# Tile places in SBUF: padded blocks of u, shifted weight halves and reused mask buffers in a hybrid SSD and retention layer

## The chip, the core and the metric

The kernel runs on one core of one Trainium2 chip. The metric is the device time of one execution in microseconds. Before the change, three executions took 860.56, 860.64 and 860.13 us, with a median of 860.56.

## What is computed

One decoder layer on a sequence of 256 tokens with a width of 1024, in fp32. Three blocks follow one another, each behind an RMS norm with a shift and a scale that are computed from a conditioning vector (`ada_w`):

```python
u = modulate(rms_norm(h, norm_ffn1_w), sh1, sc1)
h = h + 0.5 * g1 * swiglu(u, ffn1_w_in, ffn1_w_out)
u = modulate(rms_norm(h, norm_mix_w), sh2, sc2)
h = h + g2 * hybrid_mixer(u, ...)        # SSD branch and retention branch, gated and summed
u = modulate(rms_norm(h, norm_ffn2_w), sh3, sc3)
h = h + 0.5 * g3 * swiglu(u, ffn2_w_in, ffn2_w_out)
out = rms_norm(h, norm_final_w)
```

The projections are matrix products of the 256 tokens with weights of 1024 x 5632 (both FFN inputs), 2816 x 1024 (both FFN outputs), 1024 x 13344 (the mixer's input), 2048 x 1024 twice (the branches) and 1024 x 1024 (the mixer's output).

## The kernel before

**Products.** Activations lie transposed, features on the partitions and the 256 tokens along the free axis. Each fp32 operand is split into a high and a low half of type float32r, and a product is three matmuls on TensorE (`mm3`, lines 134 to 137; `l` is the stationary operand, `r` the moving one):

```python
pe.matmul(o, l[0], r[0], ...)   # L135: high weights, high activations
pe.matmul(o, l[0], r[1], ...)   # L136: high weights, low activations
pe.matmul(o, l[1], r[0], ...)   # L137: low weights, high activations
```

A matmul loads a 128 x 128 stationary tile (a weight load, engine row PEld) and streams the moving operand past it, 256 columns here, 1024 bytes of each partition. While matmul i streams, the weights of matmul i+1 are loaded.

**Weights.** `load` (L113) fetches 1 MB into one of four staging tiles `wst` on SP's queue. `half` (L120 to L128) makes its halves: `act.copy` writes `wh` (L126) and `dve.tensor_tensor` writes `wl` (L127), each 128 x 1024, with four buffers of either (`HALF_BUFS`). All of it comes from the pool `wp`: four `wst`, four `wh`, four `wl`, in this order.

**Activations.** `new_u` (L214) makes `uh` and `ul`, the halves of u, as 8 blocks (one for each 128 features) of T + 2 = 258 columns; a block is 1032 bytes. The two columns more carry the shift, for `early_project` (L257), whose matmuls are 258 columns wide. `pair_project` (L277) is the standard projection of u: 2 tiles of 128 output features x 8 blocks x 3 matmuls. In the first FFN's opening stage (`first_mms`, L415) the loop is turned round: block kt stays for 48 matmuls (16 output tiles x 3), then the next block. In it VectorE also has the dot products of `ada_w` (L179) and the halves of weights and u (L391, L413). The FFN activations are `ah`, `alo`, 22 blocks of 1024 bytes, from a pool `fp` opened once for each FFN; the mixer's tiles of 4 blocks x 1024 bytes are `slot` (name `s`, 17 buffers), from the pool `mx`, at the same base as `fp`. `contract` (L311) multiplies `ah` or a slot with weights, `branch` (L777) a slot. In `v_tile` (L817) and in the second FFN's output (from L974) the roles are turned round: u or `ah` is stationary, `wh` and `wl` move, with 512 or 256 columns.

**Places.** A pool hands out its tiles in the order of their first use, and a later pool begins where the one before ends. In this kernel that gives these starts, in bytes modulo 256:

| tile | before |
|---|---|
| wst, wh, wl (every buffer, and every 128-column slice of them) | 96 |
| uh, block kt | 96 + 8 kt |
| ul, block kt | 160 + 8 kt |
| ah, alo of both FFNs; every block of a slot | 128 |

**Small buffers.** The SSD's tiles `xe`, `st`, `bn` (512 columns) and `ec` (two buffers) serve the steps `states`, `state`, `bc`, `mask_rows` and `back`. The retention's decay masks come in four loads of 128 x 512 into `dm`, which has one buffer (L853 to L855), and `ret_scores` multiplies by them (L862, L863). `dt_tile` has seven small tiles of its own. `wide` is a ring of five buffers of 4 KB. `square_add` (L226) keeps its sum in `ssum`, two buffers.

**Order.** The opening stage is ordered by hand (`manual_schedule`); in the mixer the string `ORDER` gives the order of the steps; inside it each engine's queue, SP's too, is laid out by the tile framework as operands and buffers come free, and then runs in order.

Of the kernel before, what the change touches and what calls it, by code (L numbers as in the profile page):

```python
# [12 lines left out]
F32 = mybir.dt.float32  # L13
F32R = mybir.dt.float32r
# [4 lines left out]
P = 128  # L19
T = 256  # L20
D = 1024
KD = D // P
FFN = 2816
NF = FFN // P
DI = 2048
NH = 32
# [8 lines left out]
V_GB, V_SN, V_RN = 216, 232, 248  # L35
V_DS, V_DTB, V_AL = 264, 280, 312
N_VEC = 344

K_ID, K_TRI, K_M = 0, 128, 256
K_INV, K_SGN = 384, 385  # L40
# [37 lines left out]
def layer(ctx: ExitStack, tc: tile.TileContext, a, out, packing):  # L78
    nc = tc.nc
# [3 lines left out]
    wp = ctx.enter_context(tc.tile_pool(name="wp", bufs=1))  # L83
    sp = ctx.enter_context(tc.tile_pool(name="sp", bufs=1))
    dp = ctx.enter_context(tc.tile_pool(name="dp", bufs=1, space=bass.MemoryType.DRAM))
    pp = ctx.enter_context(tc.tile_pool(name="pp", bufs=4, space=bass.MemoryType.PSUM))
    pm = ctx.enter_context(tc.tile_pool(name="pm", bufs=4, space=bass.MemoryType.PSUM))

    uid = [0]

    def nm(s):
        uid[0] += 1
        return f"{s}_{uid[0]}"
# [51 lines left out]
    al = slice(None)  # L145
# [23 lines left out]
    col = cst.tile([P, N_VEC], F32, name="col")  # L169
# [3 lines left out]
    h = cst.tile([P, KD, T], F32, name="h")  # L173
# [38 lines left out]
        return rs  # L212

    def new_u():  # L214
        full = [sp.tile([P, KD, T + 2], F32R, tag=n, name=nm(n), bufs=1) for n in ("uh", "ul")]
        return tuple(t[:, :, :T] for t in full) + tuple(full)

    def u_tile(u, f, t, jsh):
        sh = modc[:, jsh, f:f + 1]
# [4 lines left out]
    sums = []  # L224

    def square_add(f):  # L226
        if f == 0:
            sums[:] = [sp.tile([P, T], F32, tag="ssum", name=nm("ssum"), bufs=2)]
            act.activation(sums[0], h[:, f, :], AF.Square)
            return  # L230
        sq = sp.tile([P, T], F32, tag="sq", name=nm("sq"), bufs=2)
        act.activation(sq, h[:, f, :], AF.Square)
        if f < KD - 1:
            dve.tensor_tensor(sums[0], sums[0], sq, ALU.add)
        else:
            sums.append(sq)
# [90 lines left out]
    with (tc.tile_pool(name="ep", bufs=1) as ep,  # L327
# [5 lines left out]
        for i in range(2):  # L333
            fetch(h[:, 4 * i:4 * i + 4, :].rearrange("p f t -> p (f t)"), "x",
                  lambda m, i=i: m[:, 512 * i:512 * i + 512].T.reshape(4, P, T).transpose(1, 0, 2))
# [44 lines left out]
        am = sp.tile([P, KD], F32, tag="am", name=nm("am"), bufs=2)  # L380

        def halves(kt):
            his = [wp.tile([P, 1024], F32R, tag="wh", name=nm("wh"), bufs=HALF_BUFS) for _ in range(2)]
            los = [wp.tile([P, 1024], F32R, tag="wl", name=nm("wl"), bufs=HALF_BUFS) for _ in range(2)]
            return his, los

# [82 lines left out]
    with tc.tile_pool(name=nm("fp"), bufs=1, reuse_waits="tile") as fp:  # L469
# [43 lines left out]
        am = scale_col(V_N2, 4)  # L513
# [3 lines left out]
    with tc.tile_pool(name="mx", bufs=1, reuse_waits="tile") as mx:  # L517
# [6 lines left out]
        def small(shape, tag, bufs=1):  # L524
            return mx.tile(shape, F32, tag=tag, name=nm(tag), bufs=bufs)

        def wide(shape, dt=F32):
            return mx.tile(shape, dt, tag="m", name=nm("m"), bufs=WIDE_BUFS)
# [2 lines left out]
        bT, cT = slot([P, 4, T]), slot([P, 4, T])  # L531

        dskip = col[:, V_DS:V_DS + 16]
        dtb, ahead = col[:, V_DTB:V_DTB + NH], small([P, NH], "ahead")
        rows = dp.tile([2, NH, P], F32, name="rows")

        def conv_pair(f0, dst):
# [25 lines left out]
        def dt_tile():  # L563
            need("e")
            st = load(w_in, 0, KD, C_DT, NH)
            wd = wp.tile([P, 1024], F32R, tag="wh", name=nm("wh"), bufs=HALF_BUFS)
            wd = wd[:, :KD * 2 * NH].rearrange("p (k n) -> p k n", k=KD)
            split_into(wd[:, :, :NH], wd[:, :, NH:], st)
            ps = proj_ps()
            for kt in range(KD):  # L570
                uh, ul = at(u, al, kt)
                if kt:
                    pe.matmul(ps[:NH, 0, :], wd[:, kt, :NH], ul, start=False, stop=False)
                pe.matmul(ps[:2 * NH, 0, :], wd[:, kt, :], uh, start=kt == 0, stop=kt == KD - 1)
                if not kt:
                    pe.matmul(ps[:NH, 0, :], wd[:, kt, :NH], ul, start=False, stop=False)
            both = small([2 * NH, NH], "both")
            dve.tensor_tensor(both, ident[:2 * NH, :NH], ident[:2 * NH, NH:2 * NH], ALU.add)
            dtr = wide([2 * NH, T])
            act.copy(dtr, ps[:2 * NH, 0, :])  # L580
            ps = misc_ps()
            for c in range(2):
                pe.matmul(ps[:, c * NH:(c + 1) * NH], dtr[:, c * P:(c + 1) * P], both,
                          start=True, stop=True)
            v, e, s1, s2, pl = (small([P, 2, NH], n) for n in ("dtv", "dte_", "dts", "dts2", "dtp"))
            dve.tensor_tensor(v, ps[:, :64].rearrange("p (c h) -> p c h", c=2),
                              dtb.unsqueeze(1).broadcast_to([P] + x2), ALU.add)
            act.activation(e, v, AF.Abs)
            lookup(ahead, col[:, V_AL:V_AL + NH], AF.Exp)
            lookup(e, e, AF.Exp, scale=-1.0)  # L590
            dve.tensor_scalar(s1, e, 2.0, None, ALU.add)
            dve.reciprocal(s1, s1)
            dve.tensor_tensor(s1, s1, e, ALU.mult)
            dve.tensor_tensor(s2, s1, s1, ALU.mult)
            dve.tensor_scalar(pl, s2, 1.0 / 17, None, ALU.mult)
            for n in (15, 13, 11, 9, 7, 5, 3):
                dve.scalar_tensor_tensor(pl, pl, 1.0 / n, s2, ALU.add, ALU.mult)
            dve.scalar_tensor_tensor(pl, pl, 1.0, s1, ALU.add, ALU.mult)
            dve.tensor_scalar(v, v, 0.0, None, ALU.max)
            dve.scalar_tensor_tensor(dt, pl, 2.0, v, ALU.mult, ALU.add)  # L600
            dve.scalar_tensor_tensor(av, dt, -1.0, ahead.unsqueeze(1).broadcast_to([P] + x2),
                                     ALU.mult, ALU.mult)
# [21 lines left out]
            ps = pair_project(w_in, c0 + p2 * 256, u)  # L624
            lookup(zs[key][:, 2 * p2:2 * p2 + 2, :], ps, AF.Silu)

        bn = small([P, 4, P], "bn")
        cs, dend = small([P, 2, NH], "cs"), small([P, NH], "dend")
        cbs, states, masks = [], {}, {}

# [219 lines left out]

        def ret_scores(hd):
            if hd % 2 == 0:
                dms[hd // 2] = mx.tile([P, 2, T], F32, tag="dm", name=nm("dm"), bufs=1)  # L853
                nc.sync.dma_start(dms[hd // 2].rearrange("p h t -> p (h t)"),
                                  a["dmask"][:, hd * T:(hd + 2) * T])  # L855
            dmask = dms[hd // 2]
            q, kk = qk["q", hd // 4][:, hd % 4, :], qk["k", hd // 4][:, hd % 4, :]
            ps = misc_ps()
            pe.matmul(ps[:, :T], kk[:, :P], q, start=True, stop=True)
            pe.matmul(ps[:, T:T + P], kk[:, P:], q[:, P:], start=True, stop=True)  # L860
            sc = wide([P, T + P])
            dve.tensor_tensor(sc[:, :T], ps[:, :T], dmask[:, hd % 2, :], ALU.mult)  # L862
            dve.tensor_tensor(sc[:, T:], ps[:, T:T + P], dmask[:, hd % 2, :P], ALU.mult)  # L863
            scs[hd] = sc
# [65 lines left out]
        first = modulated(ha, u, 6, "ffn2_w_in", (0, FFN))  # L930
    table("silu_and_others")
    with tc.tile_pool(name=nm("fp"), bufs=1, reuse_waits="tile") as fp:
        ah = fp.tile([P, NF, T], F32R, name=nm("ah"))
        alo = fp.tile([P, NF, T], F32R, name=nm("al"))
        w1 = "ffn2_w_in"
        hN = fp.tile([P, 2, D], F32, name="hN")
        gb = fp.tile([P, D], F32, name="gb")
# [122 lines left out]
```

## Time and profile before

| | |
|---|---|
| median of three executions | 860.56 us |
| profiled execution | 860.98 us |
| its span, first to last instruction | 859.2 us |
| TensorE matmul busy | 846.2 us, 98% |
| VectorE busy | 668.0 us, 78% |
| ScalarE busy | 518.5 us, 60% |
| DMA | 193.14 MB, mean 225 GB/s |

A matmul's duration in the profile overlaps the next one's, so its busy share says little on how fast matmuls follow each other. That pace is read from a stretch: its length divided by the number of matmuls that start in it. A view by windows counts every matmul that is under way in the stretch, and so two more at its start, which began before.

### The profile page before, as it was taken

What the parts mean: (1) busy time and instruction counts of PE and PEld (TensorE: products, weight loads), DVE (VectorE), ACT (ScalarE), POOL (GpSimd) and SP (SyncE); (2) the same over time, 40 slices, a digit from 0 to 9 for tenths busy, and PEclk for the clock granted to TensorE, in tenths of its full rate; (3) what the DMA queues carried; (4) which work ended last, traced back from release to release, by engine and by line L of the source; (5) the groups of instructions that cost most, each with busy time, mean ns of one, the idle gap of its engine ahead of it and who ended that gap; (6) DMA issues with size and microseconds to landing.
All of it is one profiled execution on the core that took longest, in us unless ns stands there. A gap on an engine that the chain in (4) does not pass through costs nothing.

```text
span 859.2 us, 16222 instructions
## 1 busy us (share of the span) xinstructions
PE 846.2 (98%) x6734; PEld 820.4 (95%) x6734; DVE 668.0 (78%) x1002; ACT 518.5 (60%) x743; POOL 10.3 (1%) x21
## 2 busy tenths in 40 slices
PE   7999999999999999999999999999999999999996
PEld 6999999999999989899999999999999999999896
DVE  6989889886989887687897678977979975455463
ACT  6665444465897686766465568765558644545342
POOL 0000000000200010000000000000000000000000
PEclk9999999999999999999999999999999999999999
DMA  9987788984685455435657763654555785454521
GB/s 366 413 325 275 271 296 347 363 319 147 241 313 196 148 209 198 145 135 202 217 176 290 244 219 140 221 194 175 220 194 195 261 305 197 147 192 174 187 87 49
DMA packets 30587, 193.14 MB, mean 225 GB/s; under 512 B 3489, under 2 KB 4129, under 8 KB 10034
## 3 DMA queue, kind: packets, MB, share of 16 engines
q1 hardware_dynamic: 28656, 186.40, 59.6%
q0 software_dynamic: 1568, 5.28, 1.8%
q8 instruction: 52, 0.85, 0.4%
q10 hardware_dynamic: 290, 0.44, 0.1%
q14 instruction: 21, 0.17, 0.1%
HBM read 191.02 MB, written 1.08 MB: 224 GB/s over the span
## 4 chain that ended last, share of the span: by engine, by line
PE 89%; issue 4%; DVE 2%; ACT 2%; DMA 2%; DVEq 0%; ACTq 0%; POOLq 0%
PE proj L137 27%; PE proj L136 27%; PE proj L135 27%; PE misc L135 1%; PE misc L136 1%; PE misc L137 1%; DVE wl L127 1%; DMA k<-in_consts_dram 1%; ACT wh L126 1%; DMA m<-rows 1%; PE misc L727 1%; PE misc L871 1%; PE misc L203 1%; DMA h<-in_x_dram 0%; PE misc L737 0%
## 5 line engine op out<-in xcount | busy, mean ns | idle before, releaser
L126 ACT CAST wh<-wst 128x1024 fp32r<-128x1024 f32 (+1 forms) x263 | 272.9, 1040 | 266.7 <-PE proj L136 178.3
L127 DVE TENSOR_TENSOR wl<-wst,wh 128x1024 fp32r<-128x1024 f32 (+1 forms) x263 | 317.4, 1211 | 133.0 <-ACT wh L126 132.5
L137 PE MATMUL proj<-uh,wl 128*128 128x256 f32 (+1 forms) x1312 | 370.4, 282 | 0.0
L135 PE MATMUL proj<-uh,wh 128*128 128x256 f32 (+1 forms) x1312 | 370.2, 282 | 0.0
L136 PE MATMUL proj<-ul,wh 128*128 128x256 f32 (+1 forms) x1312 | 369.3, 281 | 0.0
L136 PEld LDWEIGHTS proj<-ul,wh 128*128 128x128 f32 x1312 | 248.1, 189 | 0.3 <-issue 0.2
L137 PEld LDWEIGHTS proj<-uh,wl 128*128 128x128 f32 x1312 | 248.2, 189 | 0.2 <-issue 0.2
L135 PEld LDWEIGHTS proj<-uh,wh 128*128 128x128 f32 x1312 | 247.5, 189 | 0.3 <-ACT wh L126 0.2
L135 PE MATMUL proj<-s,wh 128*128 128x256 f32 x320 | 89.9, 282 | 1.0 <-ACT s L793 0.8
L136 PE MATMUL proj<-s,wh 128*128 128x256 f32 x320 | 89.3, 279 | 0.0
L137 PE MATMUL proj<-s,wl 128*128 128x256 f32 x320 | 89.2, 279 | 0.0
L179 DVE SCALAR_TENSOR_TENSOR wst<-wst,cb 128x1024 f32<-128x1024 f32 x56 | 67.0, 1222 | 3.7 <-DMA wst<-in_ada_w_dram 3.6
L135 PEld LDWEIGHTS proj<-s,wh 128*128 128x128 f32 x320 | 60.0, 188 | 2.1 <-ACT s L793 1.6
L136 PEld LDWEIGHTS proj<-s,wh 128*128 128x128 f32 x320 | 60.2, 188 | 0.0
L137 PEld LDWEIGHTS proj<-s,wl 128*128 128x128 f32 x320 | 60.1, 188 | 0.0
L137 PE MATMUL proj<-ah,wl 128*128 128x256 f32 x176 | 49.1, 279 | 0.0
L136 PE MATMUL proj<-al,wh 128*128 128x256 f32 x176 | 49.1, 279 | 0.0
L135 PE MATMUL proj<-ah,wh 128*128 128x256 f32 x176 | 49.1, 279 | 0.0
L136 PE MATMUL proj<-wl,ah 128*128 128x256 f32 (+1 forms) x132 | 42.1, 319 | 0.0
L137 PE MATMUL proj<-wh,al 128*128 128x256 f32 (+1 forms) x132 | 42.1, 319 | 0.0
L135 PE MATMUL proj<-wh,ah 128*128 128x256 f32 (+1 forms) x132 | 42.1, 319 | 0.0
L159 ACT ACT_TABLE_LOAD x30 | 38.5, 1283 | 1.3 <-PEq L1033 0.7
(242 smaller groups left out, 1132.4 us busy)
## 6 DMA issues: line engine op xcount, KB each, us to landing
wst<-in_mix_w_in_dram SPq DMA_DIRECT2D x52, 1024.0 KB, 4.9
wst<-in_ffn_w_in_dram SPq DMA_DIRECT2D x43, 1024.0 KB, 6.5
wst<-in_ada_w_dram SPq DMA_DIRECT2D x28, 1024.0 KB, 6.3
wst<-in_ffn_w_out_dram SPq DMA_DIRECT2D x17, 1024.0 KB, 5.2
ada<-in_ada_w_dram SPq DMA_DIRECT2D x16, 512.0 KB, 12.6
wst<-in_w_br_ssd_dram SPq DMA_DIRECT2D x8, 1024.0 KB, 4.9
wst<-in_w_br_ret_dram SPq DMA_DIRECT2D x8, 1024.0 KB, 5.1
wst<-in_ffn_w_out_dram SPq DMA_DIRECT2D x6, 768.0 KB, 4.5
```

The source lines that it names most:

```text
L126: act.copy(hi, v)
L127: dve.tensor_tensor(lo, v, hi.bitcast(F32), ALU.subtract)
L135: pe.matmul(o, l[0], r[0], start=first, stop=False, skip_group_check=skip)
L136: pe.matmul(o, l[0], r[1], start=False, stop=False, skip_group_check=skip)
L137: pe.matmul(o, l[1], r[0], start=False, stop=last, skip_group_check=skip)
L159: ins = act.preload_act_table_set(name).ins
L179: dve.scalar_tensor_tensor(st[:, i, :], st[:, i, :], 1.0, cb, ALU.mult, ALU.mult, accum_out=raw[:, j, f0 + i:f0 + i + 1])
L203: pe.matmul(ps[:, :T], mean, s, start=i == 0, stop=i == len(parts) - 1)
L727: pe.matmul(py[hh * 64:hh * 64 + 64, f * T + c * P:f * T + (c + 1) * P], xd[:, c, hl * 64:hl * 64 + 64], m[c][:, hl, :], start=True, stop= ...
L871: pe.matmul(py[:, eh, :], v[:, 0, es], sc[:, :T], start=True, stop=False)
```

## The change

The places change, and with them a few tiles. `new_u` makes blocks of 320 columns (1280 bytes) and uses the first 256 or 258. The pool `sp` first hands out its small tiles and a gap of 48 words; `ssum` has one buffer. A gap of 16 words stands between the `wh` and the `wl` tiles. The second FFN's `ah` and `alo` are 24 and 16 words longer, and start behind these. `dt_tile`'s seven small tiles become views of one `wide` tile, and each of the four mask loads has a buffer of its own: `xe`, `st`, `bn` and the second `ec`. Added up, the starts modulo 256 are:

| tile | before | after |
|---|---|---|
| wh | 96 | 96 |
| wl | 96 | 160 |
| uh, block kt | 96 + 8 kt | 0 |
| ul, block kt | 160 + 8 kt | 0 |
| blocks of slots; ah, alo of the first FFN | 128 | 0 |
| ah and alo of the second FFN | 128 and 128 | 96 and 160 |

No matmul and no operation on an engine is added or left out.

```diff
+U_ROW = 320
...
+    for tag, n, bufs in (("am", KD, 2), ("g", KD, 2), ("eb", 4, 1), ("gap", 48, 1)):
+        sp.tile([P, n], F32, tag=tag, name=tag, bufs=bufs)
...
     def new_u():
-        full = [sp.tile([P, KD, T + 2], F32R, tag=n, name=nm(n), bufs=1) for n in ("uh", "ul")]
-        return tuple(t[:, :, :T] for t in full) + tuple(full)
+        full = [sp.tile([P, KD, U_ROW], F32R, tag=n, name=nm(n), bufs=1) for n in ("uh", "ul")]
+        return tuple(t[:, :, :T] for t in full) + tuple(t[:, :, :T + 2] for t in full)
...
-            sums[:] = [sp.tile([P, T], F32, tag="ssum", name=nm("ssum"), bufs=2)]
+            sums[:] = [sp.tile([P, T], F32, tag="ssum", name=nm("ssum"), bufs=1)]
...
             his = [wp.tile([P, 1024], F32R, tag="wh", name=nm("wh"), bufs=HALF_BUFS) for _ in range(2)]
+            if kt == 0:
+                wp.tile([P, 16], F32, tag="gap", name="wgap")
             los = [wp.tile([P, 1024], F32R, tag="wl", name=nm("wl"), bufs=HALF_BUFS) for _ in range(2)]
...
-        dtb, ahead = col[:, V_DTB:V_DTB + NH], small([P, NH], "ahead")
+        dtb = col[:, V_DTB:V_DTB + NH]
...
-            both = small([2 * NH, NH], "both")
+            work = wide([P, 12, NH])
+            both, ahead = work[:2 * NH, 10], work[:, 11]
...
-            v, e, s1, s2, pl = (small([P, 2, NH], n) for n in ("dtv", "dte_", "dts", "dts2", "dtp"))
+            v, e, s1, s2, pl = (work[:, 2 * i:2 * i + 2] for i in range(5))
...
-        bn = small([P, 4, P], "bn")
+        bn = small([P, 512], "bn").rearrange("p (g n) -> p g n", g=4)
...
             if hd % 2 == 0:
-                dms[hd // 2] = mx.tile([P, 2, T], F32, tag="dm", name=nm("dm"), bufs=1)
-                nc.sync.dma_start(dms[hd // 2].rearrange("p h t -> p (h t)"),
-                                  a["dmask"][:, hd * T:(hd + 2) * T])
+                dm = small([P, 512], ("xe", "st", "bn", "ec")[hd // 2], 2 if hd == 6 else 1)
+                nc.sync.dma_start(dm, a["dmask"][:, hd * T:(hd + 2) * T])
+                dms[hd // 2] = dm.rearrange("p (h t) -> p h t", h=2)
...
-        ah = fp.tile([P, NF, T], F32R, name=nm("ah"))
-        alo = fp.tile([P, NF, T], F32R, name=nm("al"))
+        ah, alo = (fp.tile([P, NF * T + n], F32R, name=nm(name))[:, n:]
+                   .rearrange("p (f t) -> p f t", f=NF) for name, n in (("ah", 24), ("al", 16)))
```

## Rows read from the trace of the kernel before

**Rows 1.** The page's part 1: busy us (share of the span), instructions

```profile
PE 846.2 (98%) x6734; PEld 820.4 (95%) x6734; DVE 668.0 (78%) x1002; ACT 518.5 (60%) x743; POOL 10.3 (1%) x21
```

**Rows 2.** Waits of PE, all: line, releaser, us in total, times, longest us

```profile
PE misc L365 <- DMA crow<-in_c_dram: 2.3, 1, 2.3
PE misc L373 <- DVE bn L376: 1.2, 1, 1.2
PE misc L435 <- DVE dg L432: 0.9, 1, 0.9
PE proj L135 <- ACT s L793: 0.8, 1, 0.8
PE misc L203 <- ACT sq L232: 0.3, 1, 0.3
PE proj L135 <- ACT s L131: 0.2, 1, 0.2
```

**Rows 3.** Groups by line and form on PE: out<-moving,stationary, count | busy us, mean ns

```profile
L137 PE MATMUL proj<-uh,wl 128*128 128x256 f32 x1280 | 361.4, 282 | 0.0
L137 PE MATMUL proj<-s,wl 128*128 128x256 f32 x320 | 89.2, 279 | 0.0
L137 PE MATMUL proj<-ah,wl 128*128 128x256 f32 x176 | 49.1, 279 | 0.0
...
L137 PE MATMUL misc<-uh,wl 128*128 128x256 f32 x64 | 18.0, 281 | 0.0
...
L137 PE MATMUL misc<-uh,wl 128*128 128x258 f32 x32 | 9.1, 284 | 0.0
```

**Rows 4.** Windows: stretch, length, busy of PE, PEld, DVE, ACT, POOL; clock, DMA

```profile
672.21:729.25 57.04, 57.04 (x482) 57.04 (x481) 42.44 (x58) 27.93 (x34) 0.00 (x0) 1.00 0.73 261
452.69:504.03 51.34, 51.34 (x434) 51.34 (x433) 38.51 (x47) 26.99 (x34) 0.00 (x0) 1.00 0.69 248
142.16:203.75 61.59, 61.59 (x530) 61.59 (x529) 49.79 (x76) 31.59 (x47) 0.00 (x0) 1.00 0.81 296
418.64:429.84 11.20, 11.20 (x98) 11.20 (x97) 9.04 (x11) 6.31 (x8) 0.00 (x0) 1.00 0.67 238
...
789.80:820.58 30.78, 30.78 (x134) 24.79 (x133) 15.06 (x14) 12.09 (x12) 0.00 (x0) 1.00 0.52 178
```

**Rows 5.** Windows of the opening stage: blocks 1, 2, 4, 5, 6 of u

```profile
22.17:27.92 5.75, 5.75 (x50) 5.75 (x49) 5.46 (x10) 3.46 (x7) 0.00 (x0) 1.00 1.03 415
27.93:33.63 5.70, 5.70 (x50) 5.70 (x49) 5.40 (x9) 4.25 (x7) 0.00 (x0) 1.00 1.03 419
...
39.40:45.05 5.65, 5.65 (x50) 5.65 (x49) 5.35 (x9) 3.70 (x6) 0.00 (x0) 1.00 1.01 409
45.06:50.84 5.78, 5.78 (x50) 5.78 (x49) 5.48 (x10) 3.69 (x6) 0.00 (x0) 1.00 1.02 418
50.85:56.51 5.66, 5.66 (x50) 5.66 (x49) 5.36 (x9) 3.70 (x6) 0.00 (x0) 1.00 0.70 252
```

**Rows 6.** Timeline of PE: first and last of dt_tile's 16 matmuls

```profile
216.22 0.28 PE L574 MATMUL proj<-uh,wh 128*64 128x256 f32 x1
...
217.97 0.28 PE L574 MATMUL proj<-uh,wh 128*64 128x256 f32 x1
```

**Rows 7.** The chain in order of time: transposes, 128 columns each

```profile
742.56 1.75 PE misc L970 x16
```

**Rows 8.** Timeline of DVE: low half of blocks 1 and 7 of u

```profile
20.74 0.43 DVE L413 TENSOR_TENSOR ul<-uf,uh 128x256 fp32r<-128x256 f32 x1 [0.30 <-ACT uh L409]
...
54.63 0.43 DVE L413 TENSOR_TENSOR ul<-uf,uh 128x256 fp32r<-128x256 f32 x1 [0.30 <-ACT uh L409]
```

**Rows 9.** Waits of SP's queue: the mask loads

```profile
SPq L854 <- DVE m L863: 15.8, 3, 5.8
```

**Rows 10.** The tile ec: its last reader, first and last start

```profile
L740 DVE TENSOR_TENSOR s<-s,ec x4: 682/688/691, 309.0 to 415.5; 128x512 f32<-128x512 f32 x4
```

**Rows 11.** The tile dm: the products with the masks, first and last start

```profile
L862 DVE TENSOR_TENSOR m<-misc,dm x8: 413/420/426, 504.9 to 582.6; 128x256 f32<-128x256 f32 x8
```

## The prediction

> **What bounds the kernel now.** I read the page's busy shares first: TensorE's matmuls fill 98% of the span, the weight loads 95%, VectorE 78%, ScalarE 60% [rows 1]. Then PE's waits: six of them, 5.7 us in all, 4.4 us of it in the first three, before the products begin [rows 2]. So the time is the number of matmuls times the pace at which they follow each other, and the change adds and removes none. The one question is whether places change the pace.
>
> The pace comes from the windows, length over matmuls started (the count less the two that were under way). The projections of u run at 57.04 us / 480 = 118.8 ns and 51.34 / 432 = 118.8 ns; the first FFN's contraction, with `ah` moving, at 61.59 / 528 = 116.65 ns; a branch, with slots moving, at 11.20 / 96 = 116.7 ns [rows 4]. [...] What differs is the place: `ah` and slots start at 128 modulo 256, every block, against weights at 96, while each block of u stands 8 bytes further than the one before.
>
> The opening stage separates place from the rest, because one block of u stays for 48 matmuls. Its windows take 5.75, 5.70, 5.65, 5.78 and 5.66 us for blocks 1, 2, 4, 5 and 6, so 119.8, 118.8, 117.7, 120.4 and 117.9 ns [rows 5]. Same code, same engines beside it, another address: up to 2.7 ns. The odd blocks, at 8 modulo 16, are the slow ones.
>
> The second part of the cause is the weight load. `dt_tile` multiplies the very same unaligned blocks of u with stationary tiles of 64 and 32 columns instead of 128; its 16 matmuls take 217.97 - 216.22 = 1.75 us for 15 steps, 116.7 ns [rows 6]. With a short weight load beside it, u has no penalty. So I read the extra 2.2 ns as the stream of u and the weight load meeting in SBUF, and 116.65 ns as the pace of 256 moving columns left alone. The second FFN's output agrees: with 512 columns for one weight load it takes 30.78 us / 132 = 233.2 ns, twice 116.6 [rows 4].
>
> [...]
>
> **The change part by part.** *u at 0 modulo 256, weights at 96 and 160.* 256-column matmuls with u moving: 1280 and 64 for each of three lines, so 4032; 258-column ones: 32 to `misc`, as many to `proj`, on three lines, so 192 [rows 3]. No row shows u at 0 against 96 or 160. Bounds for the new pace: from above the worst block, 120.4 ns [rows 5]; from below the weight load alone, which in the transposes of 128 columns paces 1.75 us / 16 = 109.4 ns [rows 7]. I take 116.65, because the two arrangements that stay the same over many matmuls (slots, `ah`) and the one with hardly a weight load all lie there. That gives (4032 + 192) x (118.8 - 116.65 = 2.15 ns) = 9.1 us less.
>
> *Slots and the first `ah`, `alo` from 128 to 0.* 320 x 3 + 176 x 3 = 1488 matmuls [rows 3], already at 116.65. I take 0. The bounds are those of u: 1488 x 3.75 = 5.6 us more, or, a third of the way down to 109.4, at 114.2 ns, 1488 x 2.45 = 3.6 us less.
>
> *Second FFN's output and `v_tile`.* Here weights move, at 96 and 160, and the stationary tiles go to 96/160 and 0. By the code these are 132 of 512 columns and 264 of 256, and 192 of 512 columns, 106 us at the paces above. Nothing tells a sign; I take 0. The bounds are 114.2 and 120.4 ns per 256 columns, so 2.2 us less to 3.4 us more.
>
> *VectorE as the cover.* In the opening stage the low half of block 1 ends at 20.74 + 0.43 = 21.17 us, 1.0 us before its first matmul, and these halves come every (54.63 - 20.74) / 6 = 5.65 us [rows 8]. At 116.65 ns a block takes 5.60 us, so the lead shrinks by 0.3 us and holds: no cost. Below 114.2 ns (5.48 us, six blocks times 0.17 us) it is used up and VectorE sets this stage.
>
> *Mask loads.* Four loads as before. Three of them now wait in SP's queue for VectorE's reads of the single `dm`, 15.8 us in all, with weight loads behind them [rows 9], yet PE waits for none of it [rows 2]; with four buffers that wait goes, and is worth 0. The new buffers' readers must be done first; `ec`, the last, is read until 415.5 + 0.7 us [rows 10], and the first product with a mask starts at 504.9 us [rows 11]. *`dt_tile` in the ring, one `ssum`, the gaps.* No instruction more; one buffer of the ring is taken earlier. At worst a wait like PE's longest in the mixer, 0.8 us [rows 2]; I take 0.
>
> **Sum.** The profiled execution took 860.98 us; less 9.1 gives 851.9. The median of the runs is 0.4 us below the profiled one, so 851.5 us.
>
> **The rivals.** *Slower: the new distance is a bad one.* Everything that moves from 0 (4224 of u, 1488 of slots and `ah`) falls into step with the weight load as the odd blocks do. At 119.8 ns, block 1's pace, u loses 4224 x 1.0 = 4.2 us and the rest 1488 x 3.15 = 4.7 us: 869.5 us. It decides from a common pace of 118.2 ns upwards, the mean over both kinds today ((4224 x 118.8 + 1488 x 116.65) / 5712). For it: the even blocks scatter too (118.8, 117.7, 117.9), so alignment is not all. Against it: the slowest rows, blocks 1 and 5, start at 8 modulo 16, and the new place never does.
>
> [...]
>
> *Faster than forecast.* 116.65 ns is itself a meeting of the two streams, in all of today's arrangements, and the new distances avoid more of it. At 114.2 ns the gain is another 5712 x 2.45 = 14.0 us: 837.5 us, where VectorE begins to bind in the opening stage. For it: the weight load alone paces 109.4 ns [rows 7]. Against it: 512 columns per load run no better than 256.
>
> **How the numbers follow.** Forecast 0.50 (about 847 to 856 us, with the bounds of the places that I set to 0), faster than that 0.22, no change 0.13, slower 0.15. So faster by over 0.2% (1.7 us, about what a measurement of this kernel can tell from no change) 0.72, same 0.13, slower 0.15. The range runs from 838, the rival's 114.2 ns, to 861, which takes in no change; it leaves out the slower case and some 0.05 below.
>
> **What would show it.** Right: windows over projections of u and over slots have one pace, near 116.7 ns; the opening stage's blocks are all alike, about 5.60 us; PE's waits stay near 6 us; the mask loads wait for nothing. Wrong: the blocks are alike but at 118 ns or more (the distance is what counts, not the alignment); u's pace unchanged with its scatter (the cause was never the place); slots below 116 ns (the third rival); or PE waits for VectorE's halves in the opening stage, the new bound.

## The result and the profile after

The changed kernel took 856.23 us, the median of six executions (854.66 to 856.98), against 860.6 us for six of the kernel before (860.1 to 861.15): a ratio of 0.9949, 95% interval 0.9939 to 0.996. It is 4.4 us faster. The forecast was 851.5 us, 9.1 us faster, so the direction was right and a good half of the gain is missing. The profiled execution took 856.98 us, the slowest of the six, and 4.0 us less than the profiled one of before.

The page's part 1 after the change; the instructions are as many as in [rows 1]:

```profile
PE 842.5 (99%) x6734; PEld 816.4 (95%) x6734; DVE 667.5 (78%) x1002; ACT 519.2 (61%) x743; POOL 10.3 (1%) x21
```

The waits of PE, the four longest of six (line, releaser, us in total, times, longest; the change moves line numbers, so `mm3` is now L139 to L141):

```profile
PE misc L369 <- DMA crow<-in_c_dram: 2.3, 1, 2.3
PE misc L377 <- DVE bn L380: 1.2, 1, 1.2
PE proj L139 <- ACT s L800: 0.8, 1, 0.8
PE misc L441 <- DVE dg L438: 0.5, 1, 0.5
...
```

With two more of 0.2 us that is 5.2 us against 5.7 [rows 2]: the kernel is bound as it was, by the pace of its matmuls. Windows of the changed kernel (columns as in [rows 4]): u in the first FFN, `ah`, u in the mixer's first part, a branch with slots, u behind it, u in the second FFN, the second FFN's first output with 512 columns:

```profile
17.89:141.54 123.65, 123.65 (x1047) 123.65 (x1046) 111.47 (x163) 70.11 (x96) 0.00 (x0) 1.00 0.85 325
141.54:204.02 62.48, 62.48 (x530) 62.48 (x529) 50.03 (x76) 31.93 (x47) 0.00 (x0) 1.00 0.78 292
228.76:287.35 58.59, 58.59 (x508) 58.59 (x508) 52.74 (x84) 49.27 (x94) 5.97 (x10) 1.00 0.69 240
439.41:450.50 11.09, 11.09 (x98) 11.09 (x97) 11.09 (x15) 5.37 (x6) 0.00 (x0) 1.00 0.68 230
450.50:500.42 49.92, 49.92 (x434) 49.92 (x433) 38.68 (x49) 26.99 (x34) 0.00 (x0) 1.00 0.71 257
668.93:725.74 56.81, 56.81 (x482) 56.81 (x481) 42.41 (x58) 27.96 (x34) 0.00 (x0) 1.00 0.73 262
786.01:816.53 30.52, 30.52 (x134) 24.81 (x133) 15.03 (x14) 12.09 (x12) 0.00 (x0) 1.00 0.53 177
```

The expected single pace near 116.7 ns is not there; there are two. In the first FFN u runs at 123.65 / 1045 = 118.3 ns and `ah` at 62.48 / 528 = 118.3 ns (before: 116.65 [rows 4]); in the second FFN u is at 56.81 / 480 = 118.4. The branch takes 11.09 / 96 = 115.5 ns and u behind it 49.92 / 432 = 115.6 (before: 116.7 and 118.8). The granted clock was 1.00 in all seven windows, as in those of [rows 4]. The opening stage's blocks are now alike, which they were not in [rows 5]:

```profile
22.26:27.94 5.68, 5.68 (x50) 5.68 (x49) 5.38 (x10) 3.14 (x7) 0.00 (x0) 1.00 1.02 422
...
39.30:44.98 5.68, 5.68 (x50) 5.68 (x49) 5.38 (x10) 3.70 (x6) 0.00 (x0) 1.00 1.00 411
...
50.66:56.34 5.68, 5.68 (x50) 5.68 (x49) 5.38 (x8) 3.70 (x6) 0.00 (x0) 1.00 0.60 212
```

5.68 / 48 = 118.3 ns, every block behind the first. And the pace changes at a seam. The timeline of PE around 500.4 us, where two score matmuls of the retention stand between two projections (start, us, engine, line, operation):

```profile
500.08 0.28 PE L139 MATMUL proj<-uh,wh 128*128 128x256 f32 x1
500.19 0.28 PE L140 MATMUL proj<-ul,wh 128*128 128x256 f32 x1
500.31 0.28 PE L141 MATMUL proj<-uh,wl 128*128 128x256 f32 x1
500.42 0.59 PE L866 MATMUL misc<-s,s 128*128 128x256 f32 x2
...
501.43 0.28 PE L139 MATMUL proj<-uh,wh 128*128 128x256 f32 x1
501.55 0.29 PE L140 MATMUL proj<-ul,wh 128*128 128x256 f32 x1
501.68 0.28 PE L141 MATMUL proj<-uh,wl 128*128 128x256 f32 x1
501.80 0.28 PE L139 MATMUL proj<-uh,wh 128*128 128x256 f32 x1
```

Three matmuls take 0.34 to 0.35 us ahead of them and 0.37 us just behind; the 18 after those, to 503.93 us, take 2.13 us, 118.3 ns each: same operand places, another pace.

**Where the 4.0 us come from.** Start to next start, added up by kind over each profiled execution, before against after: 256-column matmuls over u 481.9 to 476.6 us, the 258-column ones 24.0 to 23.8, so 5.5 us less on u; slots 113.66 to 114.46 and `ah` 61.60 to 62.48, so 1.7 us more; `v_tile` and the second FFN's output together 0.2 us less. Of the gain on u 4.4 us lie in the mixer between 204 and 500.7 us, where the pace is near 115.6 ns. The opening stage's 384 matmuls gain nothing: they take 46.6 us in both executions. Its blocks 1 to 7 gain 0.3 us, and the first one loses 0.4, where nine matmuls instead of five follow each other at 0.21 us; those behind them follow at 0.12.

### The profile page after: what moved, and what is told of

Read it like the earlier page. It is cut to its first block, busy times and chain, and to the rows that moved or that the text cites. A ratio compares the mean times of both kernels' runs of the same rounds, so it can differ in the third digit from the quotient of the medians.

```text
span 854.9 us, 16219 instructions
## 1 busy us (share of the span) xinstructions
PE 842.5 (99%) x6734; PEld 816.4 (95%) x6734; DVE 667.5 (78%) x1002; ACT 519.2 (61%) x743; POOL 10.3 (1%) x21
## 4 chain that ended last, share of the span: by engine, by line
PE 91%; issue 4%; DMA 2%; ACT 2%; DVE 1%; DVEq 0%; ACTq 0%; POOLq 0%
PE proj L139 28%; PE proj L141 27%; PE proj L140 27%; PE misc L139 1%; PE misc L141 1%; PE misc L140 1%; DMA k<-in_consts_dram 1%; DMA m<-rows 1%; PE misc L734 1%; PE misc L207 1%; PE misc L878 1%; ACT wh L130 0%; DMA h<-in_x_dram 0%; PE misc L744 0%; ACT s L171 0%
## 5 line engine op out<-in xcount | busy, mean ns | idle before, releaser
L139 PE MATMUL proj<-uh,wh 128*128 128x256 f32 (+1 forms) x1312 | 369.3, 281 | 0.0
L141 PE MATMUL proj<-uh,wl 128*128 128x256 f32 (+1 forms) x1312 | 368.0, 280 | 0.0
L141 PEld LDWEIGHTS proj<-uh,wl 128*128 128x128 f32 x1312 | 248.2, 189 | 0.2 <-issue 0.2
L139 PEld LDWEIGHTS proj<-uh,wh 128*128 128x128 f32 x1312 | 247.1, 188 | 0.3 <-ACT wh L130 0.2
L139 PE MATMUL proj<-s,wh 128*128 128x256 f32 x320 | 90.2, 283 | 1.0 <-ACT s L800 0.8
L141 PE MATMUL proj<-s,wl 128*128 128x256 f32 x320 | 89.6, 280 | 0.0
L139 PEld LDWEIGHTS proj<-s,wh 128*128 128x128 f32 x320 | 60.0, 188 | 2.1 <-ACT s L800 1.7
L141 PEld LDWEIGHTS proj<-s,wl 128*128 128x128 f32 x320 | 60.5, 189 | 0.0
L139 PE MATMUL proj<-ah,wh 128*128 128x256 f32 x176 | 49.5, 281 | 0.0
L141 PE MATMUL proj<-ah,wl 128*128 128x256 f32 x176 | 49.4, 281 | 0.0
L139 PE MATMUL proj<-wh,ah 128*128 128x256 f32 (+1 forms) x132 | 42.1, 319 | 0.0
L141 PE MATMUL proj<-wh,al 128*128 128x256 f32 (+1 forms) x132 | 41.8, 317 | 0.0
```

What stands on the lines that cost most here:

```text
L139: pe.matmul(o, l[0], r[0], start=first, stop=False, skip_group_check=skip)
L141: pe.matmul(o, l[1], r[0], start=False, stop=last, skip_group_check=skip)
```

## The experiments

All edits below are against the changed kernel. First came the question which part of the change acts, and whether alignment or distance does. "Distance" is the start of the moving operand less the start of `wh`, modulo 256; the second number of a pair is the start of `wl` less that of `wh`. So slots and `ah` before were at 32/0, and everything that moves is now at 160/64.

**The small buffers alone.** All large places as before:

```diff
-U_ROW = 320
+U_ROW = 258
...
-    for tag, n, bufs in (("am", KD, 2), ("g", KD, 2), ("eb", 4, 1), ("gap", 48, 1)):
-        sp.tile([P, n], F32, tag=tag, name=tag, bufs=bufs)
...
-            if kt == 0:
-                wp.tile([P, 16], F32, tag="gap", name="wgap")
...
-                   .rearrange("p (f t) -> p f t", f=NF) for name, n in (("ah", 24), ("al", 16)))
+                   .rearrange("p (f t) -> p f t", f=NF) for name, n in (("ah", 0), ("al", 0)))
```

> The small buffers alone (four mask buffers, dt_tile's tiles in the ring, one ssum), all large places as before: wh, wl at 96, blocks of u at 96 and 160 plus 8 kt, slots and ah at 128. If the places carry the whole change: 860.6 us within 0.8, u at 118.8 ns, slots and ah at 116.7 ns. If the small buffers carry part of the 4.4 us (three waits of SP's queue fewer): 856 to 859 us at the same paces.

Measured: 860.2 us, ratio 0.9997 (0.9988 to 1.0007). u again takes 57.23 / 481 = 119.0 ns and `ah` 61.59 / 528 = 116.65. Mask loads, `dt_tile`'s ring tile and `ssum` are worth nothing that this run can tell from zero; the places carry the change.

**Everything that moves at 128, `wl` back at 96**, so u, slots and `ah` all at the 32/0 that slots and `ah` had before:

```diff
-    for tag, n, bufs in (("am", KD, 2), ("g", KD, 2), ("eb", 4, 1), ("gap", 48, 1)):
+    for tag, n, bufs in (("am", KD, 2), ("g", KD, 2), ("eb", 4, 1), ("gap", 32, 1)):
...
-            if kt == 0:
-                wp.tile([P, 16], F32, tag="gap", name="wgap")
...
-                   .rearrange("p (f t) -> p f t", f=NF) for name, n in (("ah", 24), ("al", 16)))
+                   .rearrange("p (f t) -> p f t", f=NF) for name, n in (("ah", 0), ("al", 0)))
```

> Blocks of u (1280 bytes apart), slots and every ah at 128, wh and wl both at 96. Theory distance (what counts is how far the moving operand stands from the next weights; 128 to 96 is a good distance, 0 to 96 and 160 a middling one): u, slots and ah all at 116.7 ns or a little below, so 4224 x 2.15 = 9.1 us under before, 851.5 us. Theory alignment (any constant place gives u about 117.3 ns, and slots lost by something else in the change): u stays at 117.3 ns, slots and ah go back to 116.7 ns, 854.5 us.

Measured: 854.15 us, ratio 0.9922 (0.9908 to 0.9937), better than the change itself. Its windows: u in the first FFN, `ah`, u in the mixer:

```profile
56.09:140.30 84.21, 84.21 (x717) 84.21 (x716) 75.19 (x111) 44.31 (x54) 0.00 (x0) 1.00 0.82 299
140.30:202.49 62.19, 62.19 (x530) 62.19 (x529) 49.90 (x76) 31.66 (x47) 0.00 (x0) 1.00 0.80 294
449.78:500.18 50.40, 50.40 (x434) 50.40 (x433) 38.58 (x47) 26.98 (x34) 0.00 (x0) 1.00 0.69 254
```

117.8, 117.8 and 116.7 ns. `ah` stands modulo 256 just where it stood before, against the same weights, and takes 62.19 us instead of 61.59 [rows 4]. So a place does not have one pace: what I had taken from slots and `ah` as the pace of a place was one of its paces. Neither expectation held: the time is near that of the alignment theory, 854.5 us, but the paces are those of neither.

**`wl` back at 96 alone**, u, slots and `ah` at 0 (160/0):

```diff
-    for tag, n, bufs in (("am", KD, 2), ("g", KD, 2), ("eb", 4, 1), ("gap", 48, 1)):
+    for tag, n, bufs in (("am", KD, 2), ("g", KD, 2), ("eb", 4, 1), ("gap", 64, 1)):
...
-            if kt == 0:
-                wp.tile([P, 16], F32, tag="gap", name="wgap")
```

> The changed kernel with wl back at 96, so that wh and wl both stand at 96 and u, slots and ah at 0. If the shift of wl to 160 is what cost slots and ah 1.0 and 1.7 ns: they are back at 116.7 ns, and the time is 853.8 to 854.5 us. If it is the distance from 0 to 96: they stay near 118 ns, and the time is 856.2 us or, where 160 was chosen well, above it, up to 860 us.

Measured: 859.71 us, ratio 0.9989 (0.9975 to 1.0003). Its ten executions lie between 856.44 and 862.43 us; nineteen of the kernel before, on the same chip, between 859.79 and 861.26. The profiled one is the 856.44 of them, with stretches at two paces (u in the first FFN, and in the second):

```profile
56.15:139.57 83.42, 83.42 (x712) 83.42 (x712) 74.75 (x110) 43.59 (x54) 0.00 (x0) 1.00 0.82 301
740.30:785.75 45.45, 45.45 (x385) 45.45 (x384) 23.39 (x23) 22.33 (x27) 0.00 (x0) 1.00 0.50 178
```

711 and 383 matmuls start in them behind the first: 117.3 and 118.7 ns. Slots and `ah` did not go back to 116.7 ns (`ah` runs at 117.3), so the shift of `wl` is not all that cost them their pace. By the medians that shift was worth 3.5 us of the change's 4.4, but the fastest execution at 160/0 lies among those of the change.

**Everything at 96** (0/0):

```diff
-    for tag, n, bufs in (("am", KD, 2), ("g", KD, 2), ("eb", 4, 1), ("gap", 48, 1)):
+    for tag, n, bufs in (("am", KD, 2), ("g", KD, 2), ("eb", 4, 1), ("gap", 24, 1)):
...
-            if kt == 0:
-                wp.tile([P, 16], F32, tag="gap", name="wgap")
...
-                   .rearrange("p (f t) -> p f t", f=NF) for name, n in (("ah", 24), ("al", 16)))
+                   .rearrange("p (f t) -> p f t", f=NF) for name, n in (("ah", 0), ("al", 0)))
```

> Everything at 96: blocks of u, slots, every ah, wh and wl, so that the distance is 0. Theory distance: as block 0 of u did in the opening stage of the kernel before (uh at 96 beside weights at 96, 119.2 ns and, once periodic, 120.0), all of u, slots and ah at 119 to 120 ns, so 5700 x 1.5 to 2 over the mean of 118.2: 865 to 871 us. Theory alignment: u 117.3, slots and ah 116.7 to 118 ns, 854 to 857 us.

Measured: 867.66 us, ratio 1.0084 (1.0067 to 1.0101), slower than before. Its windows: `ah`, u in the mixer, 512 columns in the second FFN:

```profile
142.68:206.04 63.36, 63.36 (x530) 63.36 (x529) 50.07 (x76) 31.90 (x47) 0.00 (x0) 1.00 0.77 288
456.53:508.37 51.84, 51.84 (x434) 51.84 (x433) 38.11 (x47) 26.90 (x34) 0.00 (x0) 1.00 0.66 242
796.95:826.90 29.95, 29.95 (x134) 24.78 (x133) 14.98 (x14) 12.11 (x12) 0.00 (x0) 1.00 0.54 178
```

63.36 / 528 and 51.84 / 432 are both 120.0 ns, as the theory of distance expected, and so is every other long stretch of 256 columns. Each block is aligned here as in the change, so alignment is not what pays: with it the blocks become alike, at whatever pace the distance gives (118.3 ns in the change, 120.0 here). The 512-column matmuls gain at the same time (226.9 ns, before 233.2 [rows 4]): a place that was bad for 256 columns was good for 512. The weights move in these, but the role is not what decides: the 256-column matmuls of the same output, weights moving too, stay at 120.0 ns here.

**A row of matmuls alone.** A kernel that computes nothing of the layer: three matmuls as in `mm3`, twelve times over, for each distance of the moving operand (0 to 240 in steps of 16) and of `wl` (0 to 224 in steps of 32), and each pair three times: right behind the last, behind one 512-column matmul, behind a 128-column matmul of fp32, a form that the trace shows as two (`ones` by `ones` in the kernel before, L352: eleven in the code, 22 in the trace). No other engine has work then. Further rows of the same kernel move all operands together, and exchange the roles at 512 columns.

```diff
...
+        for lo in range(0, 64, 8):
+            for d in range(0, 64, 4):
+                for n in range(3):
+                    kick(n)
+                    triples(12, d, 0, (0, lo))
...
```

> None of the layer is computed here: the kernel is a row of matmuls alone, groups of 36 (12 of the three-matmul products, 256 columns), with no other engine at work. The distance from wh to the moving operand goes through 0 to 240 bytes in steps of 16, that from wh to wl through 0 to 224 in steps of 32, and each pair runs three times: straight on, behind a 512-column matmul, and behind two 128-column fp32 ones. At the end some pairs repeat with both weights moved by 32, 64 and 96 bytes. Theory rhythm (the two streams lock into one of a few periodic patterns, which the distances allow and the interruption before the group picks): the pairs of the kernels run so far show their paces here too: 120.0 ns at 0/0; 116.7 and 117.8 at 32/0; 117.3 and 118.7 at 160/0; 115.6 and 118.3 at 160/64; and some pairs give different paces behind different interruptions. Theory other engines (the scatter within one kernel comes from what ScalarE, VectorE and DMA do beside): one pace for each pair, the same behind all three. Shifting everything together changes nothing if distances alone count.

Measured at 256 columns over the last 23 steps of each row of 36, in ns (distance/`wl`, the three repetitions):

| pair | where | ns |
|---|---|---|
| 0/0 | all at 96 | 120.0, 120.0, 120.0 |
| 32/0 | slots, `ah` before | 116.7, 116.8, 116.8 |
| 160/0 | `wl` back at 96 | 118.8, 118.7, 118.9 |
| 160/64 | the change | 118.5, 118.3, 118.3 |
| 192/0 | | 113.3, 117.8, 113.3 |
| 64/128 | | 113.3, 118.9, 113.3 |
| 192/128 | | 113.3, 113.3, 113.3 |
| 96/224 | the worst | 124.7, 124.7, 117.7 |

Windows of that kernel, from the 13th matmul of a row to its last start: 0/0 once, 64/0 twice (behind nothing, and behind the 512-column matmul), 160/64 once, 192/128 once:

```profile
42.15:44.91 2.76, 2.76 (x25) 2.76 (x24) 0.00 (x0) 0.00 (x0) 0.00 (x0) 1.00 0.00 0
...
90.49:93.09 2.61, 2.61 (x25) 2.61 (x24) 0.00 (x0) 0.00 (x0) 0.00 (x0) 1.00 0.00 0
94.85:97.56 2.71, 2.71 (x25) 2.71 (x24) 0.00 (x0) 0.00 (x0) 0.00 (x0) 1.00 0.00 0
...
597.14:599.86 2.72, 2.72 (x25) 2.72 (x24) 0.00 (x0) 0.00 (x0) 0.00 (x0) 1.00 0.00 0
...
1046.48:1049.09 2.61, 2.61 (x25) 2.61 (x24) 0.00 (x0) 0.00 (x0) 0.00 (x0) 1.00 0.00 0
```

Length over 23 gives 120.0, 113.5, 117.8, 118.3 and 113.5 ns. VectorE, ScalarE and GpSimd stand at 0.00 and DMA at 0, and most paces of the layer are there all the same, 113.3, 116.7, 117.8, 118.3, 118.9 and 120.0 ns: no other engine is needed for them. The rhythm theory of the expectation held in part. At 64/0 the same matmuls at the same places run at two paces, and the difference is what ran just before; 36 of the 128 pairs differ by more than 0.5 ns between their repetitions. But 160/0 does not show the layer's 117.3 ns, nor 160/64 its 115.6. Moving all operands by 32, 64 or 96 bytes together left 120.0 at 0/0 (and 120.0 to 120.2 at 96/0), and 116.5 to 117.8 at 32/0, the two paces that the layer has there: it is the distance that counts. With the roles exchanged 512 columns take 226.6 to 235.7 ns by place, 227.4 at 0/0. Nor do busy engines change the 120.0 ns at 0/0: it is the same here, with none of them at work, and in the layer, beside 50.07 us of VectorE and 31.90 of ScalarE in 63.36 us, and DMA at 288 GB/s.

**Theory from here on: a rhythm.** This is my reading of the paces above; no view shows where the two streams meet. At a given distance the moving stream and the weight loads fall into one of a few repeating patterns; an interruption (a stall, another kind of matmul, the border of a stage) picks which, and it holds until the next. Then 192/128, one of three pairs with the low pace in all three repetitions (112/0 and 16/128 are the others), should do best in the layer, and pairs with two paces should show both.

**192/128 in the layer**: u, slots and `ah` at 32, `wl` at 224:

```diff
-    for tag, n, bufs in (("am", KD, 2), ("g", KD, 2), ("eb", 4, 1), ("gap", 48, 1)):
+    for tag, n, bufs in (("am", KD, 2), ("g", KD, 2), ("eb", 4, 1), ("gap", 40, 1)):
...
-                wp.tile([P, 16], F32, tag="gap", name="wgap")
+                wp.tile([P, 32], F32, tag="gap", name="wgap")
...
-                   .rearrange("p (f t) -> p f t", f=NF) for name, n in (("ah", 24), ("al", 16)))
+                   .rearrange("p (f t) -> p f t", f=NF) for name, n in (("ah", 16), ("al", 0)))
```

> The changed kernel with other places: u, slots and the first ah at 32, wh at 96, wl at 224, the second FFN's ah and alo at 96; so u stands 192 behind wh and wl 128 behind wh, a pair that ran at 113.3 ns in the row of matmuls after all three interruptions. Theory rhythm: u, slots and ah at 113.3 to 113.6 ns over whole stretches; from before, 4224 x 5.4 + 1488 x 3.3 = 28 us less, 832.5 us, and up to 5 us of that given back where VectorE's halves become the bound (opening stage): 832 to 838 us. If the row of matmuls does not stand for the kernel (the other engines disturb, and each interruption throws it into 117.7 ns): 850 to 855 us.

Measured: 840.09 us (838.53 to 840.79), ratio 0.9763 (0.9749 to 0.9778): faster than both kernels, though 2.1 us above the 838 expected at most. Its windows (u in the first FFN, in the mixer, in the second FFN, and 512 columns):

```profile
56.40:136.99 80.58, 80.58 (x712) 80.58 (x712) 72.46 (x109) 43.56 (x54) 0.00 (x0) 1.00 0.83 300
...
443.46:492.42 48.96, 48.96 (x434) 48.96 (x433) 38.99 (x49) 26.98 (x34) 0.00 (x0) 1.00 0.72 264
657.42:711.84 54.42, 54.42 (x482) 54.42 (x481) 42.34 (x58) 27.97 (x34) 0.00 (x0) 1.00 0.75 272
769.78:800.57 30.79, 30.79 (x134) 24.79 (x133) 15.07 (x14) 12.05 (x12) 0.00 (x0) 1.00 0.52 181
```

48.96 / 432 = 113.3 ns, and 113.3 to 113.4 in the others: in every long stretch of 256 columns with u, slots or `ah` moving the pace that the row alone has. The opening stage hardly gains by it. Its blocks 1 to 3:

```profile
21.37:26.81 5.44, 5.44 (x50) 5.44 (x49) 5.14 (x9) 3.67 (x6) 0.00 (x0) 1.00 1.02 413
26.81:32.25 5.44, 5.44 (x50) 5.44 (x49) 5.14 (x8) 3.59 (x6) 0.00 (x0) 1.00 1.02 414
32.25:37.87 5.62, 5.62 (x50) 5.56 (x49) 5.32 (x9) 3.69 (x6) 0.00 (x0) 1.00 1.03 419
```

Two blocks go through at 5.44 us (113.3 ns); the third begins with a gap of 0.14 us, and blocks 3 to 6 take 5.62, 5.63, 5.77 and 5.60 us, 5.66 on average. That is the rate of VectorE's low halves of u, and in each of these blocks the second matmul, the first that reads `ul`, starts 0.05 us after VectorE has ended that block's half (32.39 and 32.34 us in block 3). The tile `ul` in the same run, first and last start:

```profile
L419 DVE TENSOR_TENSOR ul<-uf,uh x8: 424/426/427, 15.0 to 54.6; 128x256 fp32r<-128x256 f32 x8
```

39.6 / 7 = 5.66 us, as in [rows 8]. Blocks 1 to 7 together take 39.45 us, after the change 7 x 5.68 = 39.76; at 113.3 ns throughout they would take 38.1. New among PE's waits is also one for `wl`, in the first FFN's contraction:

```profile
PE proj L141 <- DVE wl L131: 1.3, 3, 0.8
```

So part of the gain becomes waits for VectorE. These three did not change the pace: `ah` is at 113.3 ns ahead of the first (137.1 to 154.8 us) and behind the last (178.1 to 197.9).

**192/0 in the layer**: u, slots and `ah` at 32, `wl` at 96:

```diff
-    for tag, n, bufs in (("am", KD, 2), ("g", KD, 2), ("eb", 4, 1), ("gap", 48, 1)):
+    for tag, n, bufs in (("am", KD, 2), ("g", KD, 2), ("eb", 4, 1), ("gap", 8, 1)):
...
-            if kt == 0:
-                wp.tile([P, 16], F32, tag="gap", name="wgap")
...
-                   .rearrange("p (f t) -> p f t", f=NF) for name, n in (("ah", 24), ("al", 16)))
+                   .rearrange("p (f t) -> p f t", f=NF) for name, n in (("ah", 16), ("al", 0)))
```

> As d32wl224 with wl at 96: distance 192, wl 0 behind wh, a pair that ran at 113.3, 117.8 and 113.3 ns after the three interruptions. Theory rhythm: within one execution some stretches at 113.3 and others at 117.8 ns, the change falling on an interruption, so anything from 834 to 856 us, and executions that differ by several us, as those with u at 0 and wl at 96 did. Theory of one pace for each place: all stretches of u alike, executions within 1 us.

Measured: 846.38 us, ratio 0.9835 (0.9821 to 0.985). The two paces of the row alone, 113.3 and 117.8, stand side by side. Windows of the same contraction of `ah`, first and second part, and the timeline of PE between them:

```profile
137.04:167.00 29.96, 29.96 (x267) 29.96 (x266) 25.89 (x41) 13.27 (x19) 0.00 (x0) 1.00 0.94 342
173.34:198.43 25.09, 25.09 (x214) 25.09 (x214) 18.43 (x27) 14.12 (x22) 0.00 (x0) 1.00 0.67 251
```

```profile
172.40 0.28 PE L139 MATMUL proj<-ah,wh 128*128 128x256 f32 x1
172.52 0.28 PE L140 MATMUL proj<-al,wh 128*128 128x256 f32 x1
173.12 0.38 PE L141 MATMUL proj<-ah,wl 128*128 128x256 f32 x1 [0.32 <-DVE wl L131]
173.34 0.28 PE L139 MATMUL proj<-ah,wh 128*128 128x256 f32 x1
173.46 0.28 PE L140 MATMUL proj<-al,wh 128*128 128x256 f32 x1
173.57 0.28 PE L141 MATMUL proj<-ah,wl 128*128 128x256 f32 x1
```

113 ns up to 172.5 us (29.96 us for 264 or 265 matmuls); then one wait of 0.32 us for VectorE; then 25.09 / 213 = 117.8 ns to the end of the stage, from the first matmuls on. Operands and places are those from before the wait. VectorE and DMA are less busy behind it (18.43 of 25.09 us and 251 GB/s, against 25.89 of 29.96 and 342), but the row alone had both paces at 192/0 with either idle. The stall itself costs 173.34 - 172.52 less two steps, 0.6 us; the pace that it leaves behind 213 x 4.45 ns = 0.9 us.

**64/128 in the layer**: u, slots and `ah` at 160, `wl` at 224:

```diff
-    for tag, n, bufs in (("am", KD, 2), ("g", KD, 2), ("eb", 4, 1), ("gap", 48, 1)):
+    for tag, n, bufs in (("am", KD, 2), ("g", KD, 2), ("eb", 4, 1), ("gap", 8, 1)):
...
-                wp.tile([P, 16], F32, tag="gap", name="wgap")
+                wp.tile([P, 32], F32, tag="gap", name="wgap")
...
-                   .rearrange("p (f t) -> p f t", f=NF) for name, n in (("ah", 24), ("al", 16)))
+                   .rearrange("p (f t) -> p f t", f=NF) for name, n in (("ah", 48), ("al", 0)))
```

> u, slots and the first ah at 160, wh at 96, wl at 224: distance 64, wl 128 behind, a pair that ran at 113.3, 118.9 and 113.3 ns. Theory rhythm: stretches at 113.3 and at 118.9 ns side by side, 834 to 862 us, executions apart by several us. Theory of one pace for each place: as for the run before.

Measured: 854.26 us, ratio 0.9929 (0.9912 to 0.9946): 118.89 ns in the first FFN and most of the mixer, 113.34 in the second FFN. Windows in the two FFNs:

```profile
56.09:144.90 88.81, 88.81 (x749) 88.81 (x749) 79.22 (x116) 46.53 (x57) 0.00 (x0) 1.00 0.81 296
...
741.58:779.65 38.07, 38.07 (x338) 38.07 (x337) 21.03 (x20) 19.27 (x22) 0.00 (x0) 1.00 0.53 189
```

88.81 / 747 and 38.07 / 336: again the two paces that the row alone showed for this pair, 118.9 and 113.3. The rhythm theory's other sign, executions several us apart, did not come: the four lie within 1.4 us here, and within 2.8 at 192/0.

**Narrow stationary tiles, alone.** This tests the sentence of the prediction that a short weight load leaves the moving columns alone. The row of matmuls again, none of the layer, with stationary tiles of 32, 64 and 128 columns:

```diff
...
+        for c in (32, 64, 128):
+            for d in (0, 8, 16, 28, 40, 48):
...
+                    narrow(16, d, c)
...
```

> A row of matmuls alone again, none of the layer. First part: wh and wl at one place, the stationary tile 32, 64 or 128 columns wide, the moving operand 0, 32, 64, 112, 160 or 192 bytes behind, 48 matmuls after each of the three interruptions. If 116.7 ns is what 256 moving columns take alone, as the prediction had it: 32 and 64 columns run at 116.7 ns at every distance, and only 128 columns differ by distance (120.0 at 0, 113.3 or 117.8 at 64 and 192). If the pace is made by the meeting with the weight load and nothing else: the narrower the tile, the lower the pace, towards 109 ns at 32 columns, and no distance matters there. Second part, with the roles of the second FFN's output (weights move, 256 columns; the stationary tile 0 to 224 bytes behind; wl 0 or 128 behind wh): some distance below the 117.3 ns that the changed kernel has there.

Measured: with 32 columns 113.3 to 120.0 ns, with 64 113.3 to 120.1, with 128 113.3 to 120.0, by distance. At distance 32 the narrowest tile takes 117.3 to 120.0, worse than the full one (116.7 to 117.8). No width went below 113.3. Neither expectation held: narrow tiles have no single pace, and none near 109 ns. In the second part, with weights moving, 47 of the 48 rows take 116.8 to 120.2 ns and one 113.3 (64/0, behind the 512-column matmul only), so no place is clearly below 117.3 in all three repetitions.

## Where the prediction held and where it failed, by its steps

**What bounds the kernel, and that the blocks of u differ by their address: right.** PE waits for 5.2 us, and with all blocks at one place the scatter of [rows 5] is gone.

**The pace of u: the step that failed.** "I take 116.65, because the two arrangements that stay the same over many matmuls (slots, `ah`) and the one with hardly a weight load all lie there." u runs at 118.3 ns in both FFNs and at 115.6 in much of the mixer. Its term came to 5.5 us instead of 9.1, 1.3 ns a matmul instead of 2.15. The size rested on a reading that three runs take apart. 116.65 ns is not the pace of 256 columns left alone: at 192/128 they take 113.3 with a full weight load beside each (712 of 128 x 128, 0.19 us each, in the window with 712 matmuls). It isn't even the pace of its own place: with everything at 128 `ah` takes 117.8. And the agreement of `dt_tile` [rows 6] said nothing of short weight loads, since 32 columns give 113.3 to 120.0 by distance; nor was 233 ns the constant of 512 columns, which take 226.9 at 0/0. That the stream of u and the weight load meet, and that the load alone sets the 109.4 ns of the transposes [rows 7], the bound from below, were my estimates; no run shows either, and in the row alone no width of the stationary tile went below 113.3.

That the time fell at all was in part luck. An estimate from these paces: with u at 118.3 ns throughout, u would have gained 4224 x 0.5 = 2.1 us and slots and `ah` at 118.3 lost 1488 x 1.65 = 2.5 us, so no gain. The gain came from the stretch of the mixer at 115.6 ns, a second pace that no step of the prediction has.

**Slots and `ah`: mis-sized.** "I take 0"; they cost 1.7 us, from 116.65 towards 118.3. That was inside the bound that I had given (5.6 us more). The second FFN's output and `v_tile`, set to 0, came to 0.2 us less; the 264 matmuls of 256 columns among them ran near 118.4 ns before, not at the 116.65 that the bounds of this term go by. The three together explain the miss in the profiled execution: 3.6 + 1.7 - 0.2 = 5.1 us, and 856.98 - 851.9 = 5.1.

**The rivals.** "No change" had 0.13. A common pace near 118.2 ns, at which u's gain is paid by slots and `ah`, is what the first FFN shows, at 118.3, and u in the second is at 118.4; the prediction's own sign of being wrong, blocks alike but at 118 ns or more, came with 5.68 us a block. "Faster than forecast" was right that another place can lower the 116.65, though that this pace is a meeting of two streams was an estimate; the change itself goes only to 115.56, in part of the mixer. What it could have given is the run at 192/128: 840.1 us, against the 837.5 worked out for 114.2 ns. "Slower" did not happen here, but its price is real one place further: with everything at distance 0 the pace is 120.0 ns and the time 867.7 us (869.5 worked out for 119.8). That places might not matter at all is ruled out: kernels with the same 6734 matmuls and as many weight loads take 840 and 868 us, and differ in places alone. Whether the moving operand and the weight load share a path, and which part of it, no run here shows.

**The cover.** VectorE's lead in the opening stage held at 118.3 ns, and at 113.3, below the 114.2 named in the prediction, it was used up by block 3.

**The mask loads: worth nothing, though not without waits.** The prediction had said that they would wait for nothing. The waits of SP's queue after the change:

```profile
SPq L861 <- DVE s L747: 8.0, 1, 8.0
...
SPq L861 <- PE misc L695: 0.8, 1, 0.8
...
SPq L861 <- PE misc L744: 0.5, 1, 0.5
```

The 15.8 us behind `dm` [rows 9] are gone, and 9.3 us behind the last readers of `xe`, `st`, `bn` and `ec` have come. PE waits for none of it, before or after.

**What stays open.** Why a distance has just these paces, and which of them a given interruption picks: the stall at 173.1 us shows a switch, and the row alone shows that the matmul ahead matters, but three waits at 192/128 switched nothing, and no run chose a pace on purpose in the changed kernel. The row alone did not show the change's own 115.56 ns either. The pairs 112/0 and 16/128, 113.3 ns (16/128 up to 113.7) in all three repetitions, weren't tried in the layer. That places count modulo 256 bytes and not by another period was taken for granted; no run tested it.

## What to carry to other kernels

Where PE is bound by matmuls with a new weight load each, the starts of the moving and the stationary operand, given here modulo 256 bytes, are a parameter: the same layer took 840 to 868 us by them alone; sweep their distance with a row of matmuls alone, behind different neighbours, and take a pair that is fast behind all of them. One such pair was tried in the layer here, and it held. A pace read from one stage was that stage's pace and no constant of its place (`ah` at 32/0: 116.65 ns before, 117.8 with everything at 128), so it did not carry over to a new arrangement. Count what the faster pace then runs into: here VectorE took back most of what the opening stage would have gained, 1.4 of 1.7 us.

## What the runs showed of the hardware that was not expected

The pace of 256-column float32r matmuls took a few values. Long stretches of the layer stood at 113.33, 115.56, 116.67, 117.33, 117.78, 118.33, 118.67, 118.89 or 120.0 ns, each constant to some 0.1 ns over hundreds of matmuls. Six of them, 113.33, 115.56, 116.67, 117.78, 118.89 and 120.0, lie one or two steps of 1.11 ns apart; the other three (117.33, 118.33, 118.67) do not fit that, and no run shows what sets the step.

The 213 matmuls behind one stall of 0.32 us, at 192/0, took 4% longer each than those ahead of it. Executions of one kernel spread by 6.0 us over ten at 160/0, 2.3 us over six for the change, 1.5 us over nineteen for the kernel before. That the paces make this spread is not shown: 192/128, with one pace, spread by 2.3 us over four executions, and 64/128, with two, by 1.4.
